# The prelude of a hybrid attention block written as one listed order of steps, its first modulation in two column halves

## The chip, the cores and the metric

The kernel runs on one core of a Trainium2 chip. The metric is the device time of one execution in microseconds; a time is the median of the runs shown. Each engine of the core executes its own instructions strictly in the order of the program: PE (TensorE: matrix products), DVE (VectorE) and ACT (ScalarE) (elementwise work), POOL (GpSimd), and SP, which here only issues DMA transfers. They meet at semaphores.

## The reference, cut to what matters

One block of width 1024 over a sequence of 1024 tokens. All of it is computed in float32.

```python
mod = jax.nn.silu(c) @ w_mod[l] + b_mod[l]          # 1024 -> 6 * 1024
shift1, scale1, gate1, shift2, scale2, gate2 = jnp.split(mod, N_MOD, axis=-1)
u = modulate(rms_norm(h, ln1_g[l]), shift1, scale1)  # xn * (1 + scale1) + shift1
mix = token_mixer(u, w_in[l], ...)                   # proj = u @ w_in, attention and RWKV branches
h = h + gate1[:, None, :] * mix
u2 = modulate(rms_norm(h, ln2_g[l]), shift2, scale2)
h = h + gate2[:, None, :] * conv_ffn(u2, ...)
```

`proj = u @ w_in` holds, among much else, two blocks of 128 columns for the low-rank parts of the RWKV branch (`xw`, `xa` in one block, `xg` in the other). They are the first products taken of `u`.

## The kernel before, in words

Nearly everything past the start is matrix products. A float32 product with enough precision is made of three products in a rounded format: each operand is split in an upper part `hi` (a cast on ACT) and a rest `lo` (a subtraction on DVE), and `hi*hi`, `hi*lo` and `lo*hi` are summed in PSUM. The bulk of the kernel is woven by a small planner (`Weave`) which interleaves projections with the chains of the two branches.

The **prelude** is what runs before that: from `x` and `c` to `u` and to the two low-rank blocks. It works on eight column tiles `kt` of 128 columns of the width, and on two halves of 512 tokens. Inside it SP, DVE and ACT execute in the order of the code, as PE always does. Its steps before:

- `load_x` and `mod_load` issue the loads: 8 tiles of `x`, then 8 row tiles [128, 1024] of `w_mod` for segment 1 (the scale) into 4 buffers `mw`, then 8 for segment 0 (the shift) into those and into the buffers of `x`, then the two low-rank weights `raw_in` (`low_w`).
- `square`, `norm_x`: ACT sums the squares of each token tile; DVE builds `dg`, diagonal matrices of the reciprocal norms.
- `turn`: PE transposes and normalises `x` with products against `dg`, 16 groups of 4 (`tr`); ACT copies each from PSUM to `uf`.
- `mod_add`: DVE forms `acc = sum over kt of sc[kt] * w_mod[kt]`, 8 instructions of [128, 1024] for each segment; `mod_sum` reduces `acc` over partitions with 8 PE products against a column of ones (`mps`) and makes `m1` (shift and scale) and `A1` (scale times gain).
- `warm(n)`: n PE products into a tile `idle` whose result nobody reads; they fill PE's time.
- `u_steps`: for each half and `kt`, DVE applies `A1` and `m1` to `uf`, ACT casts `u_hi`, DVE subtracts `u_lo`.
- `low_part`: the low-rank products, 2 weights x 3 parts x 8 `kt` x 2 halves = 96 PE products (`low`), half 0 first, and within a half the parts 0 and 1 for each `kt` and then part 2 for all.
- `low_out`: the two results leave PSUM through ACT (`sh_low`) and DVE (`xwa`, `xg`).

After it come the first projection weights (`load_w`: `raw_in`, `hi_in`, `lo_in`), their products `ps_rkv`, and the second low-rank products `zp`, which read the split `xs` of `xwa`.

Of the kernel before, what the change touches and what calls it, by code (L numbers as in the profile page):

```python
# [17 lines left out]
KT = 8  # L18
# [27 lines left out]
NC2 = CST["blk"][0]  # L46

# [85 lines left out]
def hybrid_block(ctx: ExitStack, tc: tile.TileContext, a, out):  # L133
# [122 lines left out]
    def load_w(src, name, pool=None, n=1024, scale=None, tags=("whi", "wlo"), bufs=2):  # L256

        pool = pool or wp
        raw = rp.tile([128, n], F32, tag="raw", name=f"raw_{name}")
        nc.sync.dma_start(raw, src)  # L260
        if scale is not None:
            nc.gpsimd.tensor_tensor(raw, raw, scale, op=ALU.mult)
        hi = pool.tile([128, n], F32R, tag=tags[0], name=f"hi_{name}", bufs=bufs)
        lo = pool.tile([128, n], F32R, tag=tags[1], name=f"lo_{name}", bufs=bufs)
        if weave.late == 1:
            i = nc.gpsimd.tensor_copy(hi, raw)
            if "head" in marks:
                tc.add_manual_dep(i.ins, marks["head"].ins.name, NOSYNC)
            late_lo.append((hi, lo, raw))
            weave.spawn(lower(9000), 0)  # L270
        else:
            nc.scalar.copy(hi, raw)  # L272
            for c in range(0, n, NH):
                nc.vector.tensor_tensor(lo[:, c : c + NH], raw[:, c : c + NH], f32(hi[:, c : c + NH]), op=ALU.subtract)  # L274
        return hi, lo
# [70 lines left out]
    with ExitStack() as es:  # L346
# [66 lines left out]
        with tc.tile_pool(name="st", bufs=1) as st, tc.tile_pool(name="stp", bufs=2, space=PS) as stp, \  # L413
                tc.manual_schedule(engines={mybir.EngineType.SP, mybir.EngineType.DVE, mybir.EngineType.Activation}):
            ssq = st.tile([128, 8], F32, name="ssq")
            rstd = st.tile([128, 8], F32, name="rstd")
# [8 lines left out]
            def square(half, xs, js):  # L425
                for j in js:
                    t = half * 4 + j
                    nc.scalar.activation(uf[1][:, 6:8, :].rearrange("p k s -> p (k s)"), xs[j], AF.Square,
                                         accum_out=ssq[:, t : t + 1])

            def norm_x(half):

                hs = slice(half * 4, half * 4 + 4)
                rms_rstd(rstd[:, hs], ssq[:, hs])
                for j in range(half * 4, half * 4 + 4):
                    ts(dg[:, j, :], ident, rstd[:, j : j + 1], None, op0=ALU.mult)

            def mod_load(i, tags):
                ws = [st.tile([128, D], F32, tag=tags[kt % len(tags)], name=f"wm{i}{kt}", bufs={"mw": 4, "xt": 8}[tags[kt % len(tags)]])
                      for kt in range(KT)]  # L440
                for kt, w in enumerate(ws):
                    nc.sync.dma_start(w, a["w_mod"][kt * 128 : kt * 128 + 128, i * D : i * D + D])
                return ws, st.tile([128, D], F32, name=f"acc{i}")
# [6 lines left out]
            def mod_add(kt, ws, acc):  # L450
                if kt == 0:
                    ts(acc, ws[kt], sc[:, 0:1], None, op0=ALU.mult)
                else:
                    stt(acc, ws[kt], sc[:, kt : kt + 1], acc, op0=ALU.mult, op1=ALU.add)

            def mod_sum(i, acc):
                for j0 in (0, 4):
                    ps = stp.tile([128, 4], F32, tag="mp", name=f"mps{i}{j0}")
                    for j in range(4):
                        c0 = (j0 + j) * 128  # L460
                        mm(ps[:, j : j + 1], acc[:, c0 : c0 + 128], ones[:, 0:1], start=True, stop=True)
                    tt(m1[:, i * 8 + j0 : i * 8 + j0 + 4], ps, V("b_mod", i * 8 + j0, 4), op=ALU.add)
                    if i == 1:
                        stt(A1[:, j0 : j0 + 4], m1[:, 8 + j0 : 12 + j0], 1.0, V("ln1_g", j0, 4), op0=ALU.add, op1=ALU.mult)

            def turn(kt, half, xs):
                ps = stp.tile([128, NH], F32, tag="tp", name=f"tr{half}_{kt}")
                for j in range(4):
                    mm(ps[:, j * 128 : j * 128 + 128], xs[j][:, kt * 128 : kt * 128 + 128], dg[:, half * 4 + j, :], start=True, stop=True)
                return ps  # L470

            def u_steps(half):

                cs = slice(half * NH, half * NH + NH)
                for kt in range(KT + 1):
                    if kt < KT:
                        x = uf[half][:, kt, :]
                        ts(x, x, A1[:, kt : kt + 1], m1[:, kt : kt + 1], op0=ALU.mult, op1=ALU.add)
                        nc.scalar.copy(u_hi[:, kt, cs], x)
                    if kt > 0:  # L480
                        k = kt - 1
                        tt(u_lo[:, k, cs], uf[half][:, k, :], f32(u_hi[:, k, cs]), op=ALU.subtract)
                        yield k

            def low_part(kt, half, parts):
                for (wh, wl), ps in zip(low, low_ps):
                    for i in parts:
                        w, x = ((wh, u_hi), (wh, u_lo), (wl, u_hi))[i]
                        mm(ps[half], w[:, kt * 128 : kt * 128 + 128], x[:, kt, half * NH : half * NH + NH],
                           start=kt == 0 and i == 0, stop=kt == KT - 1 and i == 2)  # L490
# [20 lines left out]
            idle = pb.tile([128, NH], F32, tag="big", name="idle")  # L511
            xs = [load_x(half) for half in range(2)]
            m = [mod_load(1, ("mw",)), None]
            uf = [st.tile([128, KT, NH], F32, name=f"uf{half}") for half in range(2)]
            warm(28)
            for half in range(2):
                square(half, xs[half], range(4))
                norm_x(half)
            for half in range(2):
                for kt in range(KT):  # L520
                    nc.scalar.copy(uf[half][:, kt, :], turn(kt, half, xs[half]))
# [15 lines left out]
            for raw, hi, _ in low_raw:  # L537
                nc.scalar.copy(hi, raw)
            low_ps = [[stp.tile([128, NH], F32, tag=("low", "tp")[hf], name=f"low{j}{hf}") for hf in range(2)] for j in range(2)]
            for half in range(2):  # L540
                for kt in u_steps(half):
                    low_part(kt, half, (0, 1))
                    if half == 0 and kt in (3, 5):
                        raw, hi, lo = low_raw[kt == 5]
                        tt(lo, raw, f32(hi), op=ALU.subtract)
                for kt in range(KT):
                    low_part(kt, half, (2,))
# [1467 lines left out]
```

## Time and profile before

| | before |
|---|---|
| times of 3 runs | 1662.81, 1658.86, 1663.45 us; median 1662.81 |
| the profiled execution | 1662.01 us, its span 1660.2 us |
| granted TensorE clock, mean | 0.989 |
| busy, share of the span | PE 97%, DVE 74%, ACT 50%, POOL 8% |

The prelude is the first 73.5 us. By stretches of 20 us (busy us of each engine, granted clock, share of the DMA engines):

| stretch | PE | DVE | ACT | PE clock | DMA |
|---|---|---|---|---|---|
| 0 to 20 | 10.97 | 4.64 | 15.00 | 1.00 | 0.89 |
| 20 to 40 | 19.91 | 15.09 | 7.03 | 0.91 | 0.96 |
| 40 to 60 | 17.22 | 16.66 | 8.09 | 0.83 | 0.28 |
| 60 to 80 | 20.00 | 14.19 | 12.55 | 1.00 | 0.50 |
| 80 to 100 | 20.00 | 16.86 | 11.56 | 1.00 | 0.88 |

A busy PE in the prelude is not all useful: 28, 40 and 6 of its products go to `idle`. "Clock" is the share of full speed that PE was granted. In the profile's lines a start and a duration come first, then engine, source line, operation, output <- inputs, count, and in brackets the idle time before it and what ended that.

### The profile page before, as it was taken

Reading aid. Unit: us, or ns where it says so; the run is one execution under the profiler, and the core shown is the slowest. Engines: PE = TensorE matmul, PEld = TensorE weight load, DVE = VectorE, ACT = ScalarE, POOL = GpSimd, SP = SyncE. Lnnn points to the kernel's source line nnn. Section 1 sums busy time; section 2 is a strip of 40 time slices with the busy share of each in tenths; the row PEclk is TensorE's granted clock in tenths of the full one; section 3 lists DMA queues with packets and bytes.
Section 4 is the critical chain, followed back from the end, with each engine's and each line's share of the span. In section 5 each row is a group of like instructions: output and inputs, shape, how many; then the busy total and the mean of one; then the engine's idle time right before and its main releaser. Section 6 shows DMA issues by size and latency. Waiting matters only on the chain.

```text
span 1660.2 us, 25947 instructions
## 1 busy us (share of the span) xinstructions
PE 1615.2 (97%) x9694; PEld 1346.1 (81%) x9694; DVE 1223.2 (74%) x2371; ACT 822.3 (50%) x1540; POOL 130.3 (8%) x152
## 2 busy tenths in 40 slices
PE   7999999999999999999999999999999999999998
PEld 7777777898978788888778887888888888888886
DVE  5786787878876536888678347897777777786677
ACT  5563335444455656666623225654444444555455
POOL 0011001111111011221022000000000000000000
PEclk9999999999999999999999999999999999999999
DMA  8488645443343246433187411243223223574363
GB/s 336 139 322 238 177 116 140 131 121 97 100 115 97 96 129 153 124 114 110 64 323 265 166 70 58 66 138 108 96 95 120 97 96 108 208 266 156 125 209 108
DMA packets 121645, 240.59 MB, mean 145 GB/s; under 512 B 40048, under 2 KB 48880, under 8 KB 121520
## 3 DMA queue, kind: packets, MB, share of 16 engines
q1 hardware_dynamic: 113040, 220.58, 40.7%
q0 software_dynamic: 8480, 18.37, 4.2%
q8 instruction: 76, 1.25, 0.3%
q14 instruction: 49, 0.40, 0.1%
HBM read 173.35 MB, written 65.54 MB: 144 GB/s over the span
## 4 chain that ended last, share of the span: by engine, by line
PE 62%; DVE 3%; ACT 2%; DMA 1%; issue 1%; SPq 0%; ACTq 0%; DVEq 0%
PE X L141 14%; PE D L141 13%; PE Y L141 7%; PE wo L141 5%; PE br L141 5%; PE gt L141 4%; PE rk_ps L141 4%; PE W L141 3%; PE lg L141 2%; PE ov L141 2%; PE tp L145 2%; DVE nm L1049 1%; DVE P L1059 1%; DMA g<-d_gate 0%; DVE tl L1089 0%
## 5 line engine op out<-in xcount | busy, mean ns | idle before, releaser
L141 PE MATMUL D<-op,op 128*128 128x512 f32 x924 | 209.8, 389 | 0.0
L141 PEld LDWEIGHTS D<-op,op 128*128 128x128 f32 x924 | 173.3, 188 | 36.3 <-DVE op L1252 0.3
L141 PE MATMUL X<-T_m,S 128*128 128x512 f32 x440 | 106.9, 389 | 0.0
L141 PEld LDWEIGHTS X<-T_m,S 128*128 128x128 f32 x440 | 82.5, 188 | 17.5 <-ACT x L1542 0.4
L1251 ACT CAST op<-g 128x512 fp32r<-128x512 f32 x77 | 47.8, 621 | 72.1 <-PE D L141 47.8
L1252 DVE TENSOR_TENSOR op<-g,op 128x512 fp32r<-128x512 f32 x77 | 53.0, 688 | 41.1 <-ACT op L1251 41.1
L1502 DVE SCALAR_TENSOR_TENSOR c<-ab,vec,c 128x512 f32<-128x512 f32 x88 | 65.9, 749 | 18.4 <-ACT c L1505 16.8
L784 DVE TENSOR_TENSOR t<-E,M 128x60 f32<-128x60 f32 (+24 forms) x248 | 56.1, 226 | 26.6 <-DMA M<-sm 20.6
L274 DVE TENSOR_TENSOR lo_in<-raw_in,hi_in 128x512 fp32r<-128x512 f32 x84 | 57.7, 725 | 22.0 <-PE gt L141 7.2
L1466 DVE TENSOR_TENSOR A<-ur,A 128x512 fp32r<-128x512 f32 x64 | 43.9, 688 | 39.0 <-ACT A L1462 38.8
L1466 DVE TENSOR_TENSOR S<-ur,S 128x512 fp32r<-128x512 f32 x66 | 45.5, 691 | 35.2 <-ACT S L1462 35.1
L1462 ACT CAST S<-ur 128x512 fp32r<-128x512 f32 x66 | 41.0, 622 | 56.1 <-DVE ur L1455 30.9
L141 PE MATMUL Y<-T_h,S 128*128 128x512 f32 x264 | 65.6, 398 | 1.6 <-ACT T_h L1720 1.0
L141 PE MATMUL Y<-T_h,A 128*128 128x512 f32 x264 | 63.4, 389 | 0.0
L1053 ACT ACTIVATE P<-lg,nm 128x896 f32<-128x896 f32 (+3 forms) x64 | 47.4, 742 | 29.3 <-DVE nm L1049 19.6
L141 PEld LDWEIGHTS Y<-T_h,S 128*128 128x128 f32 x264 | 50.6, 192 | 13.4 <-ACT T_h L1720 1.8
L1462 ACT CAST A<-ur 128x512 fp32r<-128x512 f32 x64 | 39.6, 621 | 42.9 <-PE X L141 31.0
L141 PE MATMUL W<-B_f,A 128*128 128x512 f32 x252 | 60.6, 389 | 0.0
L786 DVE TENSOR_TENSOR E<-E,t 128x60 f32<-128x60 f32 (+24 forms) x248 | 55.8, 225 | 6.4
L141 PE MATMUL X<-B_b,A 128*128 128x512 f32 x252 | 60.5, 389 | 0.0
L141 PEld LDWEIGHTS Y<-T_h,A 128*128 128x128 f32 x264 | 49.5, 188 | 10.3
L272 ACT CAST hi_in<-raw_in 128x1024 fp32r<-128x1024 f32 x42 | 43.9, 1049 | 25.4 <-PE ps_rkv L141 11.3
(481 smaller groups left out, 4142.0 us busy)
## 6 DMA issues: line engine op xcount, KB each, us to landing
raw_in<-in_w_in SPq DMA_DIRECT2D x50, 512.0 KB, 3.9
wm<-in_w_mod SPq DMA_DIRECT2D x48, 512.0 KB, 6.7
ur<-in_w_up SPq DMA_DIRECT2D x44, 512.0 KB, 4.0
g<-d_g SPq DMA_DIRECT2D x35, 512.0 KB, 3.8
d_g<-gs SPq DMA_DIRECT2D x44, 256.0 KB, 2.0
d_g<-c SPq DMA_DIRECT2D x33, 256.0 KB, 4.3
d_st<-qh SPq DMA_DIRECT2D x64, 128.0 KB, 2.4
stA<-d_st POOLq DMA_DIRECT2D x8, 1024.0 KB, 6.2
```

The costliest lines, as they stand in the source:

```text
L141: nc.tensor.matmul(o, lhsT, rhs, start=start, stop=stop, skip_group_check=more)
L145: nc.tensor.transpose(o, i, eye)
L272: nc.scalar.copy(hi, raw)
L274: nc.vector.tensor_tensor(lo[:, c : c + NH], raw[:, c : c + NH], f32(hi[:, c : c + NH]), op=ALU.subtract)
L784: tt(tv, E32[:, 0:J, s : s + 1].to_broadcast([128, J, W]), M32[:, s : s + 1, s + 1 : 32].to_broadcast([128, J, W]), op=ALU.mult)
L786: tt(E32[:, 0:J, s + 1 : 32], E32[:, 0:J, s + 1 : 32], tv, op=ALU.add)
L1053: nc.scalar.activation(e[:, 0:n], lg[:, 0:n], AF.Exp, bias=nm[:, 0:1], accum_out=nm[:, 1:2])
L1251: nc.scalar.copy(hi, src)
L1252: tt(lo, src, f32(hi), op=ALU.subtract)
L1462: nc.scalar.copy(hi, src)
L1466: tt(lo, src, f32(hi), op=ALU.subtract)
L1502: stt(c, ab[:, x + hf * NH : x + hf * NH + NH], V("conv_w", 22 * x + i), c, op0=ALU.mult, op1=ALU.add)
```

## The change

All steps of the prelude become small functions with a letter each, and a text `PRELUDE` lists the order in which they are called. A step is a letter and its indices: `q` square, `r` reciprocal norm, `d` diagonals, `t` transposition (half, kt), `c`/`C` its copy on ACT / on DVE, `a` modulation add (segment, column half, kt), `p` the same sum made by PE, `f` the last product of such a sum, `m` its result, `s`/`S` scaling of `u` on ACT / on DVE, `h` cast `u_hi`, `l` subtraction `u_lo`, `w` and `v` cast and subtraction of a low-rank weight, `x` a pair of low-rank products (half, kt, part). What differs in substance:

- The modulation is summed in halves of 512 columns: 32 tiles of [128, 512] instead of 16 of [128, 1024], in 10 buffers of their own, loaded in the order scale half 0, shift half 0, the two low-rank weights, scale half 1, shift half 1.
- 4 of the 32 sums (`p007`, `p116`, `p117`, `p017`) are 4 PE products each, added in PSUM to those of `f`; the other 28 stay on DVE. The result of a half needs 4 products `f`.
- The scaling of `u` goes to ACT for 11 of 16 tiles; 3 of 16 copies out of PSUM go to DVE.
- `u` and the low-rank products of column tiles 0 to 3, for both token halves, are listed ahead of the result of the second column half.
- The products into `idle` are 18 at the start and none later (74 before).
- The casts and subtractions of the first projection weights are held behind the last `u_hi` and `u_lo`.

```diff
+PRELUDE = """
+q0 q1 q2 q3 r0 q4 d0 t01 q5 t03 C01 q6 t00 C03 q7 a100 t02 C00 a101 r1 t04 c02 d1 t07 c04 a102 t17 c07 a103 t15
+a104 c17 t16 a105 c15 a106 w0 t14 a107 c16 v0 f10 c14 w1 t06 a000 a001 t05 c06 a002 t11 c05 a003 t12 a004 c11
...
-            nc.scalar.copy(hi, raw)
+            i = nc.scalar.copy(hi, raw)
+            if "u_hi" in marks:
+                tc.add_manual_dep(i.ins, marks["u_hi"].ins.name, NOSYNC)
...
+            def mod_load(i, c):
+                for kt in range(KT):
+                    w = wm[i, c, kt] = st.tile([128, NH], F32, tag="mw", name=f"wm{i}{c}{kt}", bufs=10)
+                    c0 = i * D + c * NH
+                    nc.sync.dma_start(w, a["w_mod"][kt * 128 : kt * 128 + 128, c0 : c0 + NH])
...
+            def mod_mm(i, c, w, x):
+                new = (i, c) not in mps
+                if new:
+                    mps[i, c] = stp.tile([128, 4], F32, tag="mp", name=f"mps{i}{c}")
                 for j in range(4):
+                    mm(mps[i, c][:, j : j + 1], w[:, j * 128 : j * 128 + 128], x, start=new and j == 0, stop=x is one and j == 3, more=True)
+
+            def mod_part(i, c, kt):
+                mod_mm(i, c, wm[i, c, kt], sc[:, kt : kt + 1])
+
+            def mod_last(i, c):
+                mod_mm(i, c, accs1[i][:, c * NH : c * NH + NH], one)
...
+            def u_scale(half, kt, on_act=True):
+                x, A, B = uf[half][:, kt, :], A1[:, kt : kt + 1], m1[:, kt : kt + 1]
+                if on_act:
+                    nc.scalar.activation(x, x, AF.Identity, scale=A, bias=B)
+                else:
+                    ts(x, x, A, B, op0=ALU.mult, op1=ALU.add)
...
             xs = [load_x(half) for half in range(2)]
-            m = [mod_load(1, ("mw",)), None]
-            warm(28)
-            for half in range(2):
-                square(half, xs[half], range(4))
-                norm_x(half)
-            for half in range(2):
-                for kt in range(KT):
-                    nc.scalar.copy(uf[half][:, kt, :], turn(kt, half, xs[half]))
-            m[1] = mod_load(0, ("xt", "mw"))
+            mod_load(1, 0)
+            mod_load(0, 0)
             low_raw = [low_w(24, wp, ("whi", "wlo"), 2), low_w(25, st, ("xt", "xt"), 8)]
+            mod_load(1, 1)
+            mod_load(0, 1)
...
-            for i in (1, 0):
-                for kt in range(KT):
-                    mod_add(kt, *m[1 - i])
-                mod_sum(i, m[1 - i][1])
-                warm((6, 40)[i])
...
+            warm(18)
+            do = dict(q=square, r=factor, d=diag, t=turn, c=u_copy, C=lambda *o: u_copy(*o, False), a=mod_add, p=mod_part, f=mod_last,
+                      m=mod_sum, s=u_scale, S=lambda *o: u_scale(*o, False), h=u_upper, l=u_lower, w=low_upper, v=low_lower, x=low_mm)
+            for o in PRELUDE.split():
+                do[o[0]](*map(int, o[1:]))
             nc.scalar.copy(w2h, w2)
```

Three places of the instruction order matter for what follows. The first is ACT where the transposed tiles are copied (`uf<-tr`) and the low-rank weights are cast (`hi_in<-raw_in`, the steps `w0` and `w1`). Before:

```order
L521 COPY uf_173<-tr_5_300 128x512
L521 COPY uf_173<-tr_6_306 128x512
L521 COPY uf_173<-tr_7_312 128x512
L538 CAST hi_in_337<-raw_in_335 128x1024
L538 CAST hi_in_341<-raw_in_339 128x1024
L479 CAST u_hi<-uf_172 128x512 x8
```

Now, on the same engine:

```order
L496 COPY uf_140<-tr_7_313 128x512
L496 COPY uf_140<-tr_5_320 128x512
L513 CAST hi_in_191<-raw_in_189 128x1024
L496 COPY uf_140<-tr_6_327 128x512
L496 COPY uf_140<-tr_4_336 128x512
L513 CAST hi_in_195<-raw_in_193 128x1024
L496 COPY uf_139<-tr_6_351 128x512
L496 COPY uf_139<-tr_5_358 128x512
```

The two casts moved from behind all 16 copies to between them; eight copies stand behind the first.

The second is DVE where a low-rank weight is split (`lo_in`, the step `v0`). Before, it stands among the scaling and splitting of `u`:

```order
L478 TENSOR_SCALAR uf_172<-uf_172,A_102,m_103 128x512
L482 TENSOR_TENSOR u_lo<-uf_172,u_hi 128x512
L545 TENSOR_TENSOR lo_in_338<-raw_in_335,hi_in_337 128x1024
L478 TENSOR_SCALAR uf_172<-uf_172,A_102,m_103 128x512
L482 TENSOR_TENSOR u_lo<-uf_172,u_hi 128x512
```

Now it stands between the last add of scale half 0 (`acc_138`) and the first of shift half 0 (`acc_137`):

```order
L466 SCALAR_TENSOR_TENSOR acc_138<-wm_169,sc,acc_138 128x512
L466 SCALAR_TENSOR_TENSOR acc_138<-wm_171,sc,acc_138 128x512
L517 TENSOR_TENSOR lo_in_192<-raw_in_189,hi_in_191 128x1024
L468 TENSOR_SCALAR acc_137<-wm_173,sc 128x512
L466 SCALAR_TENSOR_TENSOR acc_137<-wm_175,sc,acc_137 128x512
```

So the subtraction moved ahead of 20 of the 28 adds.

The third is DVE behind the prelude, where `xs`, which the first `zp` products read, is made (a cast and a subtraction for each of two row halves), among adds of a later modulation segment (`acc<-wm`). Before:

```order
L566 CAST xs_632<-xwa 64x1024
L220 TENSOR_SCALAR acc_758<-wm_0_759,sc 128x1024
L508 SCALAR_TENSOR_TENSOR xg<-low_444,omu,sh_low_604 128x512
L363 MEMSET sh_rkv_683 128x1
L567 TENSOR_TENSOR xs_632<-xwa,xs_632 64x1024
L222 SCALAR_TENSOR_TENSOR acc_758<-wm_1_775,sc,acc_758 128x1024
L363 MEMSET sh_rkv_721 128x1
L566 CAST xs_631<-xwa 64x1024
L369 SCALAR_TENSOR_TENSOR k_638<-ps_rkv_658,omu,sh_rkv_683 128x512
L222 SCALAR_TENSOR_TENSOR acc_758<-wm_2_795,sc,acc_758 128x1024
L567 TENSOR_TENSOR xs_631<-xwa,xs_631 64x1024
L274 TENSOR_TENSOR lo_in_691<-raw_in_688,hi_in_690 128x512 x2
```

Now:

```order
L588 CAST xs_634<-xwa 64x1024
L234 SCALAR_TENSOR_TENSOR acc_760<-wm_1_777,sc,acc_760 128x1024
L544 SCALAR_TENSOR_TENSOR xg<-low_426,omu,sh_low_606 128x512
L379 MEMSET sh_rkv_685 128x1
L589 TENSOR_TENSOR xs_634<-xwa,xs_634 64x1024
L588 CAST xs_633<-xwa 64x1024
L234 SCALAR_TENSOR_TENSOR acc_760<-wm_2_797,sc,acc_760 128x1024
L653 TENSOR_TENSOR wf<-wr,wf 128x8x8
L385 SCALAR_TENSOR_TENSOR k_640<-ps_rkv_660,omu,sh_rkv_685 128x512
L379 MEMSET sh_rkv_723 128x1
L288 TENSOR_TENSOR lo_in_693<-raw_in_690,hi_in_692 128x512 x2
L589 TENSOR_TENSOR xs_633<-xwa,xs_633 64x1024
```

The last `xs` moved behind the split `lo_in` of the third projection weight.

More of the change, by code (lines that the diff above doesn't have):

```diff
@@ L46 @@
 NC2 = CST["blk"][0]
+PRELUDE = """
+q0 q1 q2 q3 r0 q4 d0 t01 q5 t03 C01 q6 t00 C03 q7 a100 t02 C00 a101 r1 t04 c02 d1 t07 c04 a102 t17 c07 a103 t15
+a104 c17 t16 a105 c15 a106 w0 t14 a107 c16 v0 f10 c14 w1 t06 a000 a001 t05 c06 a002 t11 c05 a003 t12 a004 c11
+p007 a005 c12 a006 t13 m10 f00 v1 c13 t10 m00 a110 s13 a111 p116 c10 a112 h13 p117 a113 s12 x130 a114 h12 x132
+s11 a115 x120 x122 h11 S10 f11 a010 s00 a011 x110 h10 x112 m11 h00 x100 a012 x102 s02 a013 p017 h02 a014 x000
+s01 x020 a015 h01 x002 a016 x022 s03 x010 l10 h03 f01 l12 x030 l11 x012 m01 S05 x032 s04 x101 S06 x121 h05 S07
+x111 h04 S14 x050 l05 h07 x040 x042 h14 l04 x051 h06 l07 x142 s17 l14 x140 x041 l06 h17 x141 l13 s15 x071 x172
+l17 h15 x131 l01 s16 x171 x152 l15 h16 x170 l03 x151 x162 l16 x150 l00 x161 l02 x160 x031 x011 x001 x021 x061
+x060 x070 x072 x052 x062
+"""
 class Weave:
@@ L448, in warm @@
                     mm(idle[:, 0:NC1], cst[:, 0:128], cst, start=True, stop=True)
-            def mod_add(kt, ws, acc):
-                if kt == 0:
-                    ts(acc, ws[kt], sc[:, 0:1], None, op0=ALU.mult)
-                else:
[L454 to L464, printed above, removed]
```

91 lines of the change are left out of this document (45 added, 46 removed).

## The prediction

> **What bounds the kernel now.** I read the page, then PE's timeline over the first 100 us, since all that changes lies there, then what ends the other engines' waits in that stretch. The page says that PE is the bound of the whole:
>
> ```profile
> span 1660.2 us, 25947 instructions
> PE 1615.2 (97%) x9694; PEld 1346.1 (81%) x9694; DVE 1223.2 (74%) x2371; ACT 822.3 (50%) x1540; POOL 130.3 (8%) x152
> ```
>
> PE's timeline (start, duration) through the prelude:
>
> ```profile
> 6.67 6.48 PE L141 MATMUL idle<-cst 128*128 128x384 f32 x28 [6.67 <-DMA cst<-in_cst]
> 12.99 1.95 PE L141 MATMUL tr<-xwa,xt 128*128 128x128 f32 x16
> 17.30 13.06 PE L141 MATMUL tr<-xwa,xt 128*128 128x128 f32 x112 [2.36 <-ACT uf L521]
> 30.44 1.95 PE L141 MATMUL mps<-cst,acc 128*128 128x1 f32 x16
> 32.25 8.81 PE L141 MATMUL idle<-cst 128*128 128x384 f32 x40
> 42.83 2.70 PE L141 MATMUL mps<-cst,acc 128*128 128x1 f32 x16 [1.77 <-DVE acc L454]
> 47.46 0.63 PE L141 MATMUL low<-u_hi,hi_in 128*128 128x512 f32 x1
> 69.81 3.88 PE L141 MATMUL low<-u_hi,lo_in 128*128 128x512 f32 x16
> 73.53 2.01 PE L141 MATMUL ps_rkv<-u_hi,hi_in 128*128 128x512 f32 x8
> 87.39 0.39 PE L141 MATMUL zp<-xs,w2h 128*128 128x512 f32 x1
> ```
>
> Until 47 us PE fills time, waiting for the modulation; then it does the 96 low-rank products, and at 73.53 the first projection starts. I take two marks: E, the start of `ps_rkv` (73.53), and Z, the first `zp` (87.39, so E plus 13.86 of gapless products). Behind Z the program is nearly the same in both kernels and PE-bound, so the gain of the kernel is the gain of Z. The sum is made against the profiled execution (1662.01 us, 1.81 of it outside the span); the median of the three runs is 1662.81, and I put the difference onto that.
>
> PE's clock must be read with it, from the busy times by stretches (start:end, length, five engines, then the granted clock, the DMA share and GB/s):
>
> ```profile
> 33.00:35.00 2.00, 2.00 (x10) 2.00 (x9) 1.93 (x3) 0.00 (x0) 0.00 (x0) 0.63 1.01 410
> 35.00:37.00 2.00, 2.00 (x8) 2.00 (x7) 1.96 (x2) 0.00 (x0) 0.00 (x0) 0.51 1.02 412
> 44.00:45.00 1.00, 1.00 (x7) 1.00 (x6) 0.06 (x1) 0.00 (x0) 0.00 (x0) 0.50 0.00 0
> 49.00:50.00 1.00, 1.00 (x3) 0.73 (x3) 1.00 (x3) 0.62 (x1) 0.00 (x0) 0.50 0.00 0
> 51.00:52.00 1.00, 1.00 (x6) 0.83 (x5) 1.00 (x2) 0.00 (x0) 0.00 (x0) 1.00 0.00 0
> ```
>
> Twice the clock falls to half a few us after a stretch of gaps and one-column products (`mps`), and it comes back under dense products. The `mps` row at 42.83 names what the second segment ends with: DVE's last add.
>
> **The loads.** The rates of the DMA engines in slices of 2.5 us, the waits for the two low-rank weights, and two landing times:
>
> ```profile
> GB/s 58 309 393 421 413 403 411 256 310 310 244 349 405 415 415 398 74 7 3 0 0 125 244 227 8 54 356 30 301 105 177 300 305 275 205 233 300 365 374 305
> 40.97 1.04 ACT L538 CAST hi_in<-raw_in 128x1024 fp32r<-128x1024 f32 x1 [10.00 <-DMA raw_in<-in_w_in]
> 42.17 1.04 ACT L538 CAST hi_in<-raw_in 128x1024 fp32r<-128x1024 f32 x1 [0.15 <-DMA raw_in<-in_w_in]
> raw_in<-in_w_in SPq DMA_DIRECT2D x50, 512.0 KB, 3.9
> al<-d_lora SPq DMA_DIRECT2D x8, 256.0 KB, 2.7
> ```
>
> Before, `x`, 16 tiles and both weights (13.9 MB with the constants) have moved by 40.4 us (the sum of the slices), and ACT gets the second weight at 42.17: 1.8 us from the last byte to use. Now 4.5 MB of `x` and constants are through at 13.8, so the first half tile is usable at 14.45 + 1.8 = 16.2. The first weight has 16 half tiles (4.19 MB) and itself (0.52) ahead: 4.99 MB have moved by 15.0, 4.22 MB at 410 GB/s take 10.3, so 25.3, and with 1.8 us 27.1. The buffers don't hold this up: the sixteenth half tile waits for the sixth add, done at 22, when three tiles are still queued.
>
> The Trainium skill's page "DMA: Bandwidth & Descriptors" (Bandwidth) speaks against the change: it wants loads of 1 MiB and more, and fits 2.0 us plus bytes over 436e3 for each, so 2.6 us for a half tile. The 2.7 us row agrees with that for a lone load. If loads ran one at a time that would be 100 GB/s; the rows of before hold 410 with up to 8 in flight, and I cost the halving at nothing, between nothing and the 244 GB/s slice (a rival below).
>
> **DVE, the chain that decides.** Durations by form (count, total us, mean ns, idle before), and one row of the timeline:
>
> ```profile
> L454 DVE SCALAR_TENSOR_TENSOR acc<-wm,sc,acc 128x1024 f32<-128x1024 f32 x14 | 18.0, 1284 | 3.3 <-DMA wm<-in_w_mod 2.9
> L482 DVE TENSOR_TENSOR u_lo<-uf,u_hi 128x512 fp32r<-128x512 f32 x16 | 11.0, 685 | 0.6 <-ACT u_hi L479 0.5
> L478 DVE TENSOR_SCALAR uf<-uf,A,m 128x512 f32<-128x512 f32 x16 | 8.5, 541 | 0.0
> L545 DVE TENSOR_TENSOR lo_in<-raw_in,hi_in 128x1024 fp32r<-128x1024 f32 x2 | 2.4, 1215 | 0.0
> L436 DVE TENSOR_SCALAR xwa<-cst,rstd 128x128 f32<-128x128 f32 x8 | 1.7, 282 | 12.6 <-ACT rstd L299 12.6
> 18.37 5.25 DVE L454 SCALAR_TENSOR_TENSOR acc<-wm,sc,acc 128x1024 f32<-128x1024 f32 x4
> L1502 DVE SCALAR_TENSOR_TENSOR c<-ab,vec,c 128x512 f32<-128x512 f32 x88 | 65.9, 749 | 18.4 <-ACT c L1505 16.8
> L597 DVE COPY z<-zp 128x512 f32<-128x512 f32 x8 | 5.4, 679 | 3.6 <-PE zp L141 3.6
> L521 ACT COPY uf<-tr 128x512 f32<-128x512 f32 x16 | 9.3, 585 | 5.0 <-PE tr L141 5.0
> L1377 ACT ACTIVATE u_m<-tr,m,A 128x512 f32<-128x512 f32 x8 | 5.6, 780 | 0.0
> ```
>
> The adds of half width are not in this trace; the nearest row is L1502, the same operation at 512 columns, 0.749 us. Four full-width adds take 5.25 with a last one of 1.284, so they start 1.32 apart: a gap of 0.04, and 0.79 for a half. So halving is no saving: 28 adds are 4 x 0.54 + 24 x 0.79 = 21.1 us, against 2 x 0.75 + 14 x 1.32 = 20.0 before. What DVE sheds is 11 of 16 scalings (6 us), what it gains 3 copies (2.0).
>
> Walked in order: `a100` at 16.2, one copy 0.68, `a101` 0.79, diagonals 0.87, six adds 4.74: `a107` ends at 23.8. Then stands `v0`, which needs `w0` on ACT, which needs the weight at 27.1: cast until 28.1, `v0` at 28.2. DVE idles 4.4 us with the next half already landed; ACT's later copies stand behind `w0`, and PE's `t06` needs a PSUM buffer that they free, so PE has only `f10` from 22.6 to 28.9. `v0` 1.2 and `a000` to `a006` 5.3 take DVE to 34.7, `m10` and `v1` to 36.3. `m00` needs `f00`, and ahead of that PE has `t06`, `t05`, then (behind `w1` and a copy on ACT) `t11`, `t12`, `p007`, `t13`. A group `tr` is 13.06/14 = 0.93 us at full clock and, by the half clock, 1.86; four one-column products are 0.98 (half of the 1.95 row). All at full clock gives `m00` at 36.8, all at half 41.0. After a gap like that the clock has fallen in both cases above, and dense products from 47.46 on brought it back between 50 and 51, so I take half clock for `t06` and `t05` only: 38.0.
>
> The Trainium skill, "TensorE: Matmul & The Clock Gate" (Part 1, the HAM clock gate), has the gate open after a busy window of about 3.4 us and close after an idle one. By that rule the gap of 6 us must close it, as I assume. The rows agree in kind: half clock from 35 to 37, and at 44 to 50.
>
> From `m00`: six adds 4.5, one scaling 0.54, `a010`, `a011` 1.3, `m11` 0.4, five adds 3.95: 48.7. Three `u_lo` and the wait for `f01`, which stands behind the products of half 0 on PE: `m01` at 51.4 (50.0 to 54.3 by the clock). Before, the same point was 45.5 (the end of the second `mps` row), but all 96 products were still to come; now 38 of them are done or due. The rest is 58 x 0.2325 (16 take 3.72 in the rows) = 13.5, from 54.0: **E = 67.5, 6.0 earlier.**
>
> **Behind E.** DVE has 4 scalings (1.9) and 13 `u_lo` (9.5) after `m01`: done at 62.8. The second projection weight loads into a buffer that the first one's `lo_in` frees:
>
> ```profile
> 73.55 1.29 DVE L274 TENSOR_TENSOR lo_in<-raw_in,hi_in 128x512 fp32r<-128x512 f32 x2 [3.09 <-issue]
> 74.91 0.33 SPq L260 DMA_DIRECT2D raw_in<-in_w_in  x1
> 75.00 0.74 DVE L508 SCALAR_TENSOR_TENSOR xwa<-low,omu,sh_low 128x512 f32<-128x512 f32 x1
> 83.93 1.22 DVE L567 TENSOR_TENSOR xs<-xwa,xs 64x1024 fp32r<-64x1024 f32 x1
> ```
>
> That `lo_in`, free to start early before, is now held behind the last `u_lo`: 64.1; the load takes 3.9 (68.0), cast 1.05, split 1.29: 70.4, where before this split ended at 74.84. ACT's `sh_low` stand behind that cast. From the first `xwa` after it to the last `xs` DVE took 75.00 to 85.15, 10.15; now a second `xwa` (0.7) and `lo_in` of the third weight (1.3) stand in between, 12.3 with the small ones. So `xs` is ready at 82.9 and **Z = 83.0, 4.4 earlier**, where the products alone would allow 81.4: PE waits 1.6 us. PE, POOL and SP queue nothing else there that comes later. The loads of `w2` and the constants moved behind 32 tiles on SP, the last of which goes out when `a113` frees its buffer, about 41; they are used at 60.
>
> What goes at no cost: the 74 idle products (PE had nothing else), the 4 `p` (4 us of PE in its gaps; if PE were full they would be 4 us), ACT's 11 scalings (nearest row L1377, 0.78 from PSUM, so 8.6 in place of idle time; ACT ends `h16` by 59.5, ahead of DVE).
>
> **Rivals.** *The tail costs nothing* (0.2): DVE catches up before Z, or `raw_in` lands early; the gain is E's, 6.0, and with the full clock throughout 7.4: 1655.4 to 1656.8. For it: the tail has only 1.6 us to make up. Against: DVE is contiguous from 73.55 to 85.2 before.
>
> *Half loads run slow* (0.15): at the 244 GB/s slice the first weight comes at 25.3 + 4.71 MB x (1/0.244 - 1/0.41) = 33.1 and 1.8: 7.8 later, and everything behind moves with it. Z is 3.4 later than before, 1666.2; at 324 GB/s (2.7 later) it is 1661.1. Against it: those slices were buffer waits (four `mw`).
>
> *The clock stays down, slower* (0.1): PE's stream from 25 to 54 is short bursts with one-column products between. Each product at half clock costs 0.2 us (0.43 against 0.2325: the half doubles). It decides when E passes 78.5, that is with 55 of the 96 products at half clock: then Z is 92.4. With 72 of them E is 81.9, Z 95.8, and the time 1671.2. Against it: dense products brought the clock back in 3 us.
>
> *The steps don't gain at all* (0.1): `m00` at half clock throughout, `m01` 54.3 or later, Z 85.9 to 88: 1661.3 to 1663.4.
>
> **Numbers.** The forecast has 0.45: 1662.8 - 4.4 = 1658.4, by its clock bounds 1657.0 to 1661.3. What a measurement can tell from no change is 0.3%, 5 us, so below 1657.8 is faster and above 1667.8 slower: the forecast lies 0.6 us from that bound, with nearly half of its chance, 0.2, below it. Faster is that and the 0.2 of the first rival; slower is the clock rival and a little of the slow loads. The range 1653.0 to 1667.0 takes in the first rival with 2 us of unknown downstream, and the slow loads, and leaves out the clock rival.
>
> **What would show it.** Right: DVE idle some 4 us ahead of `lo_in` L517 until about 28 us; PE idle some 4 us to 28.9 and a half clock after it; `ps_rkv` near 67.5; PE waiting for `xs` ahead of the first `zp`, near 83. Wrong: the first low-rank weight cast before 25 us, half-width adds clearly under 0.7 us, `zp` with no wait, or a half clock through most `low` products.

## The result: no measurable change, and the profile after

| | before | changed | ratio, 95% interval |
|---|---|---|---|
| median of 12 runs each | 1659.49 us | 1660.85 us | 1.0006, 0.9994 to 1.0018 |
| changed kernel again, 12 runs (before 30) | 1661.37 us | 1662.32 us | 1.0012, 0.9999 to 1.0024 |
| the profiled execution | 1662.01 us | 1660.32 us | |

The ratio is estimated from all runs of the session; it is not the quotient of the two medians. The forecast was 1658.4, 4.4 us less than before; the ratio says 1 us more, with 2 us either way. So the class (no change) came out as forecast, and the 4.4 us did not come. The front of the kernel did get faster. PE's timeline of the changed kernel (start, duration, then what ended a wait):

```profile
22.42 1.05 PE L153 MATMUL mps<-cst,acc 128*128 128x1 f32 x8 [0.32 <-DVE acc L466]
29.46 3.78 PE L153 MATMUL tr<-xwa,xt 128*128 128x128 f32 x16 [5.99 <-ACT uf L496]
41.05 1.20 PE L153 MATMUL low<-u_hi,hi_in 128*128 128x512 f32 x2
...
68.80 1.98 PE L153 MATMUL ps_rkv<-u_hi,hi_in 128*128 128x512 f32 x8
...
77.86 1.97 PE L153 MATMUL ps_rkv<-u_hi,lo_in 128*128 128x512 f32 x8
82.34 3.51 PE L153 MATMUL ps_rkv<-u_hi,hi_in 128*128 128x512 f32 x8 [2.50 <-DVE sh_rkv L379]
85.69 1.32 PE L153 MATMUL ps_rkv<-u_lo,hi_in 128*128 128x512 f32 x5
86.85 0.40 PE L153 MATMUL zp<-xs,w2h 128*128 128x512 f32 x1
```

E, the start of `ps_rkv`, is at 68.80: 4.73 earlier than before. Z, the first `zp`, is at 86.85: 0.54 earlier. In between PE, which had no gap there before, waits 2.50 us ahead of its third projection, and its next eight products take 3.51 in place of 1.98: the clock has fallen (stretch, length, five engines, clock, DMA share, GB/s).

```profile
82.00:83.00 1.00, 0.66 (x2) 0.59 (x3) 1.00 (x4) 0.00 (x0) 0.23 (x1) 0.51 0.93 274
83.00:84.00 1.00, 1.00 (x4) 0.81 (x3) 0.97 (x2) 0.00 (x0) 0.00 (x0) 0.50 0.94 356
```

DVE's timeline says why. The third projection needs the PSUM bank that the first `k` frees, and this `k` stands at the end of an unbroken list (the wait's row names `sh_rkv` L379, a tiny instruction that ran beside the end of `k`):

```profile
52.96 0.16 DVE L486 TENSOR_TENSOR m<-mps,vec 128x4 f32<-128x4 f32 x1 [1.45 <-PE mps L153]
...
54.99 7.91 DVE L510 TENSOR_TENSOR u_lo<-uf,u_hi 128x512 fp32r<-128x512 f32 x13
62.83 2.88 DVE L288 TENSOR_TENSOR lo_in<-raw_in,hi_in 128x512 fp32r<-128x512 f32 x1
...
65.63 0.68 DVE L288 TENSOR_TENSOR lo_in<-raw_in,hi_in 128x512 fp32r<-128x512 f32 x1
...
71.25 1.29 DVE L288 TENSOR_TENSOR lo_in<-raw_in,hi_in 128x512 fp32r<-128x512 f32 x2 [4.70 <-ACT hi_in L284]
72.46 0.75 DVE L544 SCALAR_TENSOR_TENSOR xwa<-low,omu,sh_low 128x512 f32<-128x512 f32 x1
...
80.13 1.27 DVE L234 SCALAR_TENSOR_TENSOR acc<-wm,sc,acc 128x1024 f32<-128x1024 f32 x1
...
81.46 0.74 DVE L385 SCALAR_TENSOR_TENSOR k<-ps_rkv,omu,sh_rkv 128x512 f32<-128x512 f32 x1
```

The matching rows of before:

```profile
69.65 0.75 DVE L508 SCALAR_TENSOR_TENSOR xwa<-low,omu,sh_low 128x512 f32<-128x512 f32 x1 [0.84 <-ACT sh_low L506]
...
81.97 0.73 DVE L369 SCALAR_TENSOR_TENSOR k<-ps_rkv,omu,sh_rkv 128x512 f32<-128x512 f32 x1
82.63 1.27 DVE L222 SCALAR_TENSOR_TENSOR acc<-wm,sc,acc 128x1024 f32<-128x1024 f32 x1
```

From the second weight's `lo_in` to the end of `k` DVE took 9.15 us before (73.55 to 82.70) and takes 10.95 now (71.25 to 82.20): one `xwa`, done ahead of that `lo_in` before, and one more add of the next modulation (`acc`, before behind `k`) now stand in it. The start came 2.3 earlier, the list is 1.8 longer, so `k` is 0.5 earlier, and Z with it. Of the 4.73 us at E that leaves 0.54. `k` ends at 82.20 and PE starts at 82.34. In all eleven traces below in which PE waits there, it starts 0.14 to 0.16 us behind the end of `k`, whatever the profile names as the cause.

### The profile page after: what moved, and what is told of

Same layout as the page of the kernel before. It is cut to its first block, busy times and chain, and to the rows that moved or that the text cites. A ratio compares the mean times of both kernels' runs of the same rounds, so it can differ in the third digit from the quotient of the medians.

```text
span 1658.5 us, 25950 instructions
## 1 busy us (share of the span) xinstructions
PE 1604.9 (97%) x9670; PEld 1336.9 (81%) x9670; DVE 1221.6 (74%) x2375; ACT 828.4 (50%) x1548; POOL 131.0 (8%) x152
## 4 chain that ended last, share of the span: by engine, by line
PE 59%; DVE 5%; ACT 2%; issue 1%; DMA 1%; SPq 0%; DVEq 0%; ACTq 0%
PE X L153 13%; PE D L153 13%; PE Y L153 6%; PE wo L153 5%; PE br L153 5%; PE gt L153 4%; PE rk_ps L153 3%; PE W L153 3%; PE lg L153 2%; PE ov L153 2%; PE tp L157 2%; DVE P L1081 1%; DVE nm L1071 1%; DVE tl L1111 0%; DMA g<-d_gate 0%
## 5 line engine op out<-in xcount | busy, mean ns | idle before, releaser
L1075 ACT ACTIVATE P<-lg,nm 128x896 f32<-128x896 f32 (+3 forms) x64 | 47.5, 743 | 28.6 <-DVE nm L1071 19.6
```

The source lines that it names most:

```text
L1075: nc.scalar.activation(e[:, 0:n], lg[:, 0:n], AF.Exp, bias=nm[:, 0:1], accum_out=nm[:, 1:2])
```

## The experiments

Two theories to begin with. Mine: the gain of E is lost between E and Z, on DVE's list and on what starts it late. Rival B: Z does not matter either, since something behind it takes back what is won. (Rival A, within mine: the length of DVE's list counts, whatever starts it.) A third mark, f, is the start of the first `f` products, behind `zp`: 104.70 before, 104.29 in the changed kernel. The marks of a kernel are from one trace. Six traces have the same work up to E (both of the changed kernel, e2, e6, c1, c2), and their E lies between 67.96 and 70.47, 69.2 on average; so a difference of one or two us in E between two traces shows little. The times are compared as ratios, since the median of before itself moved between sessions (1658.52 to 1661.61). All kernels, from the changed one on:

| kernel | E | PE gap ahead of 3rd projection | Z | f | ratio to before, 95% |
|---|---|---|---|---|---|
| before | 73.53 | 0 | 87.39 | 104.70 | 1 |
| changed | 68.80 | 2.50 | 86.85 | 104.29 | 1.0006 (0.9994 to 1.0018) |
| changed, again | 67.96 | 2.5 | 86.18 | 102.52 | 1.0012 (0.9999 to 1.0024) |
| e1 no rule on splits | 70.77 | 0.19 | 85.04 | 103.46 | 0.9993 (0.9978 to 1.0008) |
| e2 w2l on DVE | 70.47 | 1.01 | 86.33 | 104.15 | 1.0007 (0.9993 to 1.0022) |
| e3 low-rank weights later | 65.15 | 2.70 | 83.54 | 99.87 | 0.9978 (0.9963 to 0.9993) |
| e4 = e1 + e3 | 68.52 | 0.19 | 82.80 | 100.36 | 0.9976 (0.9962 to 0.9990) |
| e6 adds behind k | 69.36 | 0 | 83.51 | 103.50 | 1.0015 (1.0002 to 1.0028) |
| e7 = e3 + e6 | 65.22 | 1.12 | 80.42 | 98.41 | 0.9976 (0.9963 to 0.9989) |
| e9 idle products in the gap | 71.96 | 0.94 | 87.01 | 103.92 | 1.0008 (0.9995 to 1.0020) |
| e11 p steps on DVE | 66.99 | 3.06 | 85.72 | 102.69 | 1.0011 (0.9997 to 1.0025) |
| c1 loads left out | 69.59 | 3.2 | 88.29 | 104.62 | 1.0003 (0.9991 to 1.0016) |
| c2 = c1 + e6 | 69.23 | 0 | 83.25 | 100.85 | 0.9974 (0.9963 to 0.9984) |
| e13 = e7, second sum late (7 runs) | 66.77 | 1.2 | 82.05 | 98.84 | 0.9963 (0.9948 to 0.9977) |

**e3: the stall ahead of the first low-rank split.** The list of steps, from `a106` on:

```diff
-a106 w0 t14 a107 c16 v0 f10 c14 w1 t06 a000 ... m10 f00 v1 c13 t10 m00 a110 s13 a111 p116 c10 a112
+a106 t14 a107 c16 f10 c14 t06 a000 ... m10 f00 c13 t10 m00 c10 w0 v0 w1 v1 a110 s13 a111 p116 a112
```

> The changed kernel with the two low-rank weights' casts and splits (w0 v0 w1 v1) and one copy moved in the list to behind m00. The stall of 6.6 us ahead of v0 goes: a006 ends at 28 to 29, m00 at 31 to 32 with PE at full clock, the second half is then bound by its tiles' landing (42.5 at 400 GB/s, and 1.8): m01 47.5 in place of 53.0, E = 64. The tail is as long as it was: Z = 82.3, 4.5 earlier, 1656.4 us by my theory. Rival A gives the same Z here. Rival B (lost downstream): 1660.8. If loads and not DVE set the first half's end, m01 stays near 52 and nothing is won.

DVE's stall (6.59 us) and PE's gap of 5.99 us ahead of `tr` are gone; PE's timeline of e3:

```profile
23.73 3.86 PE L152 MATMUL tr<-xwa,xt 128*128 128x128 f32 x32
...
33.90 2.68 PE L152 MATMUL mps<-sc,wm 128*128 128x1 f32 x16 [2.73 <-DMA wm<-in_w_mod]
...
78.89 3.46 PE L152 MATMUL ps_rkv<-u_hi,hi_in 128*128 128x512 f32 x8 [2.70 <-DVE sh_rkv L378]
```

32 `tr` take 3.86 there, where 16 took 3.78 in the changed kernel. `m01` comes at 49.31 (expected 47.5; PE waits for tiles until 33.90), and E and Z 1.2 later than expected, but 3.65 and 3.31 earlier than in the changed kernel, f 4.4. The time follows: 0.9978, an interval that lies below both of the changed kernel's. So the place of `w0 v0 w1 v1` in the list costs 3 to 4 us, and rival B is wrong for this gain. The gap ahead of the third projection is as it was.

**e1 and e2: what starts DVE's list late.** e1 takes out the rule; e2 moves a POOL instruction that ran beside the slow `lo_in`.

```diff
 # e1
-            i = nc.scalar.copy(hi, raw)
-            if "u_hi" in marks:
-                tc.add_manual_dep(i.ins, marks["u_hi"].ins.name, NOSYNC)
+            nc.scalar.copy(hi, raw)
 ... (the same for u_lo)
 # e2
-            nc.gpsimd.tensor_tensor(w2l, w2, f32(w2h), op=ALU.subtract)
+            nc.vector.tensor_tensor(w2l, w2, f32(w2h), op=ALU.subtract)
```

> The changed kernel without the rule that holds the first projection's splits behind the last u_hi and u_lo. My theory (the 4.7 us won at E are given back behind the prelude, because the second projection weight's buffer is freed only at 66.3 by a lo_in that the rule puts behind the last u_lo): DVE does that lo_in right after m01, about 53, the second weight is split by 66, E comes 1.2 later (70.0, DVE does the lo_in ahead of 13 u_lo), the first k is done by 80.7, PE has no gap ahead of the third projection (81.0), Z = 83.9, 3.0 earlier than in the changed kernel: 1657.9 us. Rival A (DVE's tail of some 10 us from the first xwa to k sets Z whatever the weight does): PE's gap stays, Z 86 to 87, 1660 to 1661. Rival B (what is won at Z is lost downstream, in the waits for ql and z that the changed kernel shows): Z near 84, but the time stays at 1660.8.

> The changed kernel with the split of w2 (w2l, 128x1024) on DVE in place of POOL. My theory says that the lo_in of 2.88 us was slow because POOL's w2l ran at the same time: it takes 0.7 now, the buffer is free at 64.2 (2.1 earlier), the second weight is split by 70.4, k is done by 80.1, PE's gap ahead of the third projection falls from 2.5 to 0.4 us, Z = 83.4, 3.5 earlier: 1657.4 us. Rival A (DVE's tail sets Z): with 1.2 us more work on DVE Z is 87 or later, 1661. Rival B (lost downstream): Z near 83.4, and 1660.8. If the 2.88 us have another cause than POOL, that lo_in stays at 2.9.

In e1 the gap is 0.19 and the clock stays up, as expected, but E is 2.0 later than in the changed kernel (1.2 expected) and the list starts at 70.80: the second weight lands early, and then its cast waits for a buffer. ACT's row in e1:

```profile
69.39 1.05 ACT L284 CAST hi_in<-raw_in 128x1024 fp32r<-128x1024 f32 x1 [4.86 <-PE low L153]
```

The buffer is that of a low-rank weight, free only behind its last `low` product. So in e1 and e4 the list starts 0.03 us behind E though the load was early, its 11 us against PE's 11 us for two projections: that half of my theory (an early load is worth 3 us) gave 1.8 at Z, and by its time (0.9993, 1660.4 where before is 1661.6) rival A is nearer than I am. e4, both together, gave Z 82.80 and not 79.1: there DVE waited 3.26 us for that early weight's cast, ahead of `m01`. Its ratio (0.9976, 1657.6) is that of e3 alone, 1.1 from rival A and 4.5 from my theory.

> The third and the first of these together: the low-rank weights behind m00, and no rule on the projections' splits. My theory: E = 65.2, no gap ahead of the third projection, Z = 79.1, 7.8 earlier than the changed kernel: 1653.1 us. Rival A: 1656.5 (only E's gain). Rival B: 1660.8.

In e2 the `lo_in` falls to its usual time, which shows that POOL's `w2l` made it slow. POOL's row of the changed kernel, then DVE's of e2:

```profile
61.73 3.42 POOL L584 TENSOR_TENSOR w2l<-w,w2h 128x1024 fp32r<-128x1024 f32 x1 [59.76 <-DVE u_lo L510]
```

```profile
64.53 0.68 DVE L288 TENSOR_TENSOR lo_in<-raw_in,hi_in 128x512 fp32r<-128x512 f32 x1
...
65.13 0.68 DVE L288 TENSOR_TENSOR lo_in<-raw_in,hi_in 128x512 fp32r<-128x512 f32 x1
65.73 1.22 DVE L584 TENSOR_TENSOR w2l<-w,w2h 128x1024 fp32r<-128x1024 f32 x1
```

But `m01` was 1.7 later in that execution, and the list starts at 70.72 in place of 71.25 and is 0.7 longer, since DVE waited 0.9 us in it for a tile of `wm`: Z 86.33, half a us. The 2.2 us of the collision are shown, their worth at the end is not. In all ten traces with this collision `lo_in` ends 0.54 to 0.56 us behind `w2l`, so it looks held up until POOL is done, rather than slow all along. `u_lo`, of the same form, isn't held up at the start of `w2l`; rows of e1, POOL then DVE:

```profile
64.61 3.55 POOL L580 TENSOR_TENSOR w2l<-w,w2h 128x1024 fp32r<-128x1024 f32 x1 [62.64 <-ACT w2h L566]
```

```profile
58.00 7.91 DVE L506 TENSOR_TENSOR u_lo<-uf,u_hi 128x512 fp32r<-128x512 f32 x13
```

The last two `u_lo` overlap `w2l` there by 1.3 us and keep their 0.69.

**e6 and e7: the length of DVE's list.** Three adds of the next modulation are held behind the first `k`.

```diff
+            if "k" in marks:      # marks["k"]: the first k<-ps_rkv
+                tc.add_manual_dep(i.ins, marks["k"].ins.name, NOSYNC)   # i: an add into acc
```

> The changed kernel, with three modulation adds of the next stage (acc, 128x1024, 0.75 + 1.29 + 1.27 us) held on DVE behind the first k. My theory is by now: the first k stands at the end of a list of DVE work of 11 us that starts with the second weight's lo_in (71.25), and PE's third projection needs the bank that k frees. Without the three adds k ends at 78.9 instead of 82.2, PE needs the bank at 79.7: the gap of 2.5 us and the half clock behind it (1.5 us) go, Z = 82.8, 4.1 earlier than in the changed kernel: ratio to before 0.998 (1658.5 where before is 1661.6). Rival C (the gap is set by the third weight or its cast on ACT, which end near the same time): the gap stays at 2 or more, Z 86 to 87, ratio 1.0006.

> The same edit in the kernel with the low-rank weights behind m00 (E = 65.15, Z = 83.54 there). My theory: no gap ahead of the third projection, k done at 75.4, Z = 79.0, 8.4 earlier than before: ratio 0.9950 (1653.2 where before is 1661.6). Rival C: Z 83 to 84, ratio 0.998. If Z comes early and the time does not follow, something behind Z takes it: ratio above 0.997.

In e6 the expectation for Z was met: no gap, no half clock, Z = 83.51, 3.3 earlier, although the casts on ACT did not come earlier (rival C is out). At the end nothing is won: 1.0015. e6 and e3 have the same Z, and e3 is 6 us faster. In e7 Z came at 80.42, not 79.0, with a gap of 1.12: an `xs` subtraction of 1.22 us now stands ahead of `k`, which ends at 77.23 and not 75.4. Its time is e3's (0.9976 against 0.9978), not the 0.9950 of my theory, so the 3.1 us that its Z gains on e3 bring nothing either: the last case of that expectation. In e6 2.7 of the 3.9 us won at Z are lost by f, which is 1.2 earlier than before. PE's waits and then ACT's in e6 (for whom, us in total, times, longest):

```profile
PE f L153 <- ACT z L624: 1.9, 1, 1.9
PE zp L153 <- ACT z L624: 1.2, 1, 1.2
```

```profile
ACT z L624 <- DMA d_lora<-z: 4.2, 2, 3.5
ACT hi_in L286 <- DMA raw_in<-in_w_in: 4.2, 2, 3.8
```

`z`, which frees the banks of `zp`, stands on ACT behind a cast that waits for a weight, and behind stores. So behind Z there seems to be a second limit, the transfers. The stretches 0 to 100 and 100 to 120, in before, e6 and e3:

```profile
0.00:100.00 100.00, 88.11 (x447) 76.22 (x448) 67.44 (x113) 54.22 (x85) 4.87 (x9) 0.95 0.70 247
100.00:120.00 20.00, 19.17 (x85) 13.14 (x84) 16.78 (x21) 14.61 (x22) 6.11 (x4) 1.00 1.00 391
```

```profile
0.00:100.00 100.00, 83.73 (x433) 72.28 (x434) 64.76 (x116) 61.10 (x95) 5.90 (x9) 0.93 0.73 247
100.00:120.00 20.00, 18.11 (x80) 12.27 (x79) 16.34 (x20) 12.55 (x19) 6.13 (x4) 1.00 0.97 386
```

```profile
0.00:100.00 100.00, 86.37 (x440) 74.79 (x441) 68.70 (x121) 63.17 (x98) 4.91 (x9) 0.93 0.77 266
100.00:120.00 20.00, 20.00 (x86) 13.50 (x85) 18.45 (x22) 14.31 (x21) 6.12 (x4) 1.00 0.86 323
```

By 100 us e6 has moved as much as before (24.7 MB by 247 GB/s), e3 1.9 MB more: in e3 all buffers of the prelude come free earlier, and SP issues the next loads earlier; in e6 only DVE's order behind E changed, and no load starts sooner. Over all traces with every load it is the same: 26.2 to 26.7 MB by 100 us in the four kernels that are faster than before (e3, e4, e7, e13), 24.7 to 25.5 in the others. But e6 also puts loads off itself, since the adds that it holds back free the buffers of `wm`. SP's rows for the fourth load of `wm` and the next, in the changed kernel and in e6:

```profile
75.25 6.50 SPq L230 DMA_DIRECT2D wm<-in_w_mod  x3
```

```profile
80.48 3.03 SPq L230 DMA_DIRECT2D wm<-in_w_mod  x2
```

How much of e6's loss is its own doing is not shown. e1, which closes the gap without holding adds, waits for `z` as well, 1.6 us in all between Z and f.

**c1 and c2: the transfers taken away.** Both leave out 14 of the 16 loads of `wm` for the next modulation's sums, so the sums are wrong while DVE's work stays; c1 is the changed kernel, c2 is e6.

```diff
-            w = pool.tile(shape, F32, tag=tags[1], name=f"wm{seg}_{kt}", bufs=3)[:, 0:D]
-            nc.sync.dma_start(w, a["w_mod"][kt * 128 : kt * 128 + 128, seg * D : seg * D + D])
+            if kt == 0:
+                ... (the same two lines)
```

> The changed kernel with 14 of the 16 loads of wm for the modulation sums of the next stage left out (each sum uses its first tile eight times, so its values are wrong; DVE's adds stay): 7.3 MB less to move between 67 and 118. It is the control for the next one. My theory by now: behind Z there is a second limit, the loads, which run at 410 to 420 GB/s from 97 to 117 in every kernel; in the changed kernel Z is so late (86.9) that PE hardly meets it (0.9 us of waiting for z ahead of f). So the loads left out bring 1 us: f near 103.5, ratio 1.000. Rival (the loads in that stretch are beside the point): f at 104.3 as it was, ratio 1.0006.

> The same left out in the kernel with the three adds behind k, whose Z was 83.5 but whose f came at 103.5, so 2.7 of 3.9 us were lost by then (PE waited 1.2 and 1.9 us for z on ACT, which waited for a weight and for stores). My theory: with the loads gone the gain of Z is kept: f at 100.8, 3.9 earlier than before, ratio 0.9977, 3 us faster than the control. Rival (z is late for DVE's or ACT's own work): PE still waits 2 to 3 us, f at 103, same as the control.

Without the loads the changed kernel gains nothing (1.0003), and e6 gains: 0.9974 against 1.0015, intervals apart, 0.0041 x 1660 = 6.8 us. Z's gain is kept up to f (100.85, expected 100.8), and of PE's waits one of 0.9 us is left. So the gap ahead of the third projection and the transfers are two limits close behind one another: of these edits, neither alone brings anything, and both together do. At f the difference between c2 and e6 is only 2.65 of the 6.8 us; where the rest comes from is not shown. The rate in c2's stretch:

```profile
100.00:120.00 20.00, 20.00 (x87) 13.76 (x86) 17.36 (x22) 13.37 (x20) 6.71 (x4) 1.00 0.50 148
```

c1's own expectation (1 us at f) failed: with its tiles at hand early, the scheduled adds filled DVE's list further, the gap grew to 3.2 and Z came at 88.29 (0.8 of that lateness was there at E).

**e13: the same with all the work.**

```diff
+            if seg == 5 and "z5" in marks:   # marks["z5"]: the eighth store d_lora<-z
+                tc.add_manual_dep(i.ins, marks["z5"].ins.name, NOSYNC)   # i: a load of wm
```

> The kernel with the low-rank weights behind m00 and the three adds behind k, with all its work, but the loads of the second modulation sum (4.2 MB) held on SP behind the eighth store of z (about 105), out of the stretch in which the loads run at 415 GB/s into the one behind 120, where they run at 100 to 300. My theory: the last 1.3 us between E and f come back, f at 97.0, 7.7 earlier than before, ratio 0.995 to 0.996 if nothing behind f is put off. Rival: the second sum is now late itself, and what waits for it (the end of its pool, ahead of ssq and p at 151) holds PE up: ratio 0.998 or more.

The fastest kernel here, 0.9963, but e7's interval overlaps, so no gain in time over e7 is shown. f came at 98.84 (98.41 in e7, 97.0 expected), but E was 1.55 later in this trace, ahead of the edit: from E to f it is 32.07 us in place of 33.19, most of the 1.3 us that I expected. What is left between E and Z is 1.2 us in which PE waits ahead of the third projection. The profile puts them down to a cast on ACT that ends at 78.98, but the third weight's cast had ended at 77.89, and `k` ended at 78.83, 0.14 ahead of PE's start: it is `k` again.

**e9 and e11: two prices of the prelude.** e9 puts `warm(26)` behind `f10`; e11 writes `a` for the four `p`.

> The changed kernel with 26 idle products (128x384, 0.22 us each) on PE behind f10, in the 6 us in which it waits for the first low-rank weight. My theory: they keep the clock up, so the next two groups tr take 1.95 us, not 3.78; m00 comes at 36.8 in place of 38.6, m01 at 51.2, E = 67.0, and Z is 1.8 earlier: 85.0, ratio 0.9995. Rival: DVE and the loads set m01, the clock in that place costs nothing: E 68.8 as it was, ratio 1.0006. If the idle products hold PE up, E is later than 69.

> The changed kernel with its four p steps (one-column products of a weight tile on PE) done as adds on DVE, 0.79 us each. My theory: DVE is what sets m01, so two of the four count in full (a116, a117), the other two partly, since DVE waits 1.8 and 1.5 us ahead of m00 and m01: m01 1.6 to 2.4 later, E = 70.8, Z = 88.8, ratio 1.0018. Rival (the loads set m01, DVE has room): no change, 1.0006.

In e9 the clock stays up, and 16 `tr` take 2.05 and not 3.78; `m00` comes 1.3 earlier. Then it falls elsewhere. PE's rows, and the clock, in e9:

```profile
23.45 4.76 PE L153 MATMUL idle<-cst 128*128 128x384 f32 x26
29.57 2.05 PE L153 MATMUL tr<-xwa,xt 128*128 128x128 f32 x16 [1.36 <-ACT uf L496]
...
47.07 1.44 PE L153 MATMUL mps<-sc,wm 128*128 128x1 f32 x8 [2.29 <-DMA wm<-in_w_mod]
```

```profile
48.00:56.00 8.00, 8.00 (x25) 6.74 (x26) 2.69 (x7) 1.27 (x3) 0.00 (x0) 0.50 0.33 101
```

PE waits 2.29 us for a tile, runs at half clock from 48 to 56, and E is 71.96, 3.2 later than in the changed kernel's first trace and 1.5 later than the latest of the six. The local price of the gap (1.7 us) is shown; curing it brought no gain at E here, and none is seen in the time (1.0008, where 0.9995 was expected).

e11 came out on the other side of my expectation: with the four products of a tile done on DVE, E is 66.99, 1.8 earlier than in the changed kernel's first trace and 1.0 earlier than in the earliest of the six. `m00` came at 37.49 in place of 38.55, and DVE did the added work where it had waited for PE (1.8 us ahead of `m00`, 1.45 ahead of `m01`; no wait is left there). The `p` steps therefore save nothing at E. The gap behind E grew to 3.06, f (102.69) lies between those of the changed kernel's two traces, and the time did not move.

**The changed kernel again.**

> The changed kernel once more as it is: a second trace beside the first. If the 2.6 us that the first trace lost between 151 and 163 (PE waiting 1.6 us for ql) belong to the kernel, they are there again, and the offset of some 2 us between the place of f and the time; if they are of one execution, they are gone. Ratio 1.0006 either way, within 0.0012.

The wait for `ql` at 154 is gone, so it belonged to one execution; the gap of 2.5 us is there again. This second trace ends at Z 86.18, f 102.52 and 1660.7 us of span, against 86.85, 104.29 and 1658.5 for the first: behind f, two executions of one kernel drift by 4 us against each other. So no single trace can say where 2 us behind f went.

## Why the prediction was right, and where its steps were wrong

- **Up to E the walk held.** First weight's cast at 27.88 (27.1), DVE's stall 6.59 (4.4; the adds were done at 22.4, not 23.8), half clock for `t06` and `t05` (3.78 for what takes 2.05 at full), `m00` 38.55 (38.0), `m01` 52.96 (51.4; PE waits 1.22 us for the tile of `p017`, which the walk had not), E 68.80 and 67.96 (67.5), 69.2 on average over the six traces. That DVE ended its `u_lo` at 62.90 (62.8) is luck: `m01` was 1.6 late, and 13 `u_lo` took 7.91 and not 9.5. Loads of half width ran at 386 to 400 GB/s in place of 410: the rival that they run slow is out. (Its 2.7 us at 324 GB/s should be 3.0, by the 4.71 MB that its 7.8 us go by.)
- **Its zero for the `p` steps was too low**: without them E is 1.8 us earlier than in the changed kernel's first trace, 1.0 earlier than in the earliest of the six (e11, one trace).
- **"Z = 83.0, 4.4 earlier" is the step that failed.** I put 1.6 us of waiting on `xs` ahead of `zp`. `xs` was 1.8 later than forecast, 84.66, mainly from the `lo_in` of 2.88 in place of 0.69 beside POOL's `w2l` (and 70.4 + 12.3 gives 82.7, not the 82.9 of the sum); but PE never waited for it, because it had already stopped at 79.8 for the bank that `k` frees. "`zp` with no wait" was my own sign of being wrong. I looked for what `zp` needs and not for what the projection ahead of it needs. That wait with its clock is 2.5 + 1.5 us; e6 takes both away and moves Z to 83.51.
- On the slow `lo_in`: the Trainium skill, "GPSIMD Engine Reference" (1. Specifications), says that GpSimd shares its SBUF interface with VectorE, with contention for VectorE instructions that have two SBUF inputs. The rows agree in part: `lo_in`, with two such inputs, took 2.88 beside `w2l`, and the `xwa` of before, with one input in PSUM, 0.75 while `w2l` ran (69.11 to 71.51 there). But `u_lo`, with two such inputs too, kept 0.69 beside the start of `w2l`.
- **"The gain of the kernel is the gain of Z" failed too**: e6 has Z 3.9 earlier than before and no gain, and the transfers of the stretch behind are what it meets there (c2). In the kernels that are faster (e3, e4, e7), more is loaded by 100 us; that this is what makes Z's gain last is argued from the rates, and e7's further 3.1 us at Z brought nothing over e3.
- **That the class came out right is in part luck**: 4.4 us of forecast gain were 0.6 us short of what counts as a change, and the measured gain is about none (1 us more, with 2 us either way, leaves the 4.4 out). That something behind E takes from the gain was in the prediction; its size, 1.6, should have been 4, and it was another wait.
- **The rivals.** "The tail costs nothing" is out: the tail cost all but 0.5 to 1.2 us of what was won at E. "The steps don't gain" (Z 85.9 to 88) has the right Z for another reason: it put the loss ahead of `m01`. The clock's part is the 1.5 us behind the gap, not the `low` products.
- **Left open**: the kernels with f between 0.4 and 2.2 us earlier than before (changed, again, e6, e9, e11) have ratios of 1.0006 to 1.0015, some 1 to 4 us more than f gives. Traces don't settle it, as the drift behind f is of that size: from f to the end of the span the fourteen traces take 1552.3 to 1560.8 us.

## What to carry to other kernels

When a step is made to end earlier, walk on through the in-order list of the engine that serves it: find, behind the mark, each buffer or PSUM bank that the next stage needs, and what stands ahead of its release. Then ask whether the loads of the next stage can start earlier too. Where two limits lie a few us from each other, as here, an experiment on either alone can say "no effect"; take both away before you call one harmless. A list of steps written by hand should not have a DMA-dependent step (`w0 v0`) ahead of work whose data is already there: moving it, with `w1 v1`, was the one edit that paid by itself, 3.6 us against before by its ratio (0.07% to 0.37%).

## What the runs showed of the hardware

- A DVE subtraction of 128x512 from SBUF took 2.88 us beside a POOL one of 128x1024, and 0.68 without it. It ended 0.54 to 0.56 us behind the POOL one in ten traces, and the POOL one ended 2.24 to 2.25 behind the last `u_lo` in the changed kernel, e1 and e4 (it took 3.42 to 3.55 there, and 2.40 in before, where no `u_lo` ran beside it). Read together, the two kinds seem to take turns, each held up until the other's is done.
- A gap of 2.5 us was enough for the clock to fall to 0.50, for about 3 us (82 to 85 in the changed kernel). Behind the gaps of 0.94 to 1.16 us (e2, e7, e9, e13) the next eight products took 2.06 to 2.09 us, close to their 1.98 without a gap.
- The clock also stayed at 0.50 while PE was busy by the profile without a gap: 8 us from 48 to 56 in e9, behind a wait and among one-column products. The Trainium skill, "TensorE: Matmul & The Clock Gate" (Part 1: the HAM clock gate), has the full clock back after one busy window of about 3.4 us; this row is more than twice that.
